# Down projection of a decoder step: low parts on VectorE, banks emptied by copies, late tiles, a five-step tail

## The chip, the cores and the metric

The kernel runs on one core of one Trainium2 chip. The metric is the device time of one execution in microseconds (us); of several executions the median is taken. An execution's time is a little longer than the span of its trace, which runs from the first to the last instruction.

## The reference

One decoder layer for 1024 prompt tokens and 64 sample tokens: token mixing, cross-attention and a gated convolutional FFN, each between RMSNorms. The change lies in the last matmul of the FFN and the norm and residual behind it:

```python
def conv_ffn(h, p, buf):
    ...
    gate, val = jnp.split(c, 2, axis=-1)
    y = (jax.nn.gelu(gate, approximate=True) * val) @ p['w_down']     # (1024 x 2816) @ (2816 x 1024)
    return y, ext[:, t:]
...
    y, buf_new = conv_ffn(rmsnorm(x, p['g_ffn_pre']), p, buf)
    x = x + rmsnorm(y, p['g_ffn_post'])
```

## The kernel before

The product for the prompt is done in the Strassen-Winograd way. The gated rows are a 2 x 2 matrix of blocks A11 to A22 (512 tokens by 1408), the weight is one of blocks B11 to B22 (1408 by 512), and seven block products P1 to P7 (in the code's order P1, P7, P6 and P4 by turns, P5, P2, P3) take the place of eight. Each block product has 11 steps over k, so that there are 77 steps. A step needs two factors of 128 x 512, which are sums or differences of blocks; `factors` (line 1829) makes them with `minus` (VectorE, line 1826) and splits each with `dsplit`: the high part is a rounding copy on ScalarE (line 1821), the low part is source minus high part (line 1822), on the engine that `factors` names. In each step the first factor's low part is on GpSimd (`G`), the second's on VectorE (`V`); P5 has a third split, for the samples, on GpSimd.

A step then gives 4 row tiles of 128 tokens, each three matmuls of 128x128 by 128x512 (`rows`, through `mm3`, lines 374 to 376: high x high, high x low, low x high). In P1, P5, P2 and P3 two matmuls for the sample tokens follow (`rows_s`, lines 1999 and 2000). So a step has 12 or 14 matmuls, and the stage has 12 x 77 + 2 x 44 = 1012.

Each tile adds up in one PSUM bank over its 11 steps. There are eight banks: four of kind `dtile`, three of kind `aux`, one `smp`. `BANKS` says which kind a product's tiles take. A product takes banks that an earlier product has left, so its first matmul in such a bank waits until `evac` or `evac_s` has emptied it. `evac` is a ScalarE copy for P1 and P7 (lines 2005 and 2007) and a VectorE add for the others (`plus`, line 1692); P6 has a GpSimd add behind it (line 2010). `evac_s` copies half of the sample bank on ScalarE (line 2023) and adds on VectorE.

Splits are made ahead: `run_factors` makes factors as long as the 11 pairs of buffers in `slots` suffice, which is five steps with the one in work (three in P5). Blocks come from memory by SyncE's queue: `hold` for those that stay, `stage` with five buffers for those that pass through (lines 1807 and 1814). The stage has no order by hand beyond the program's: a scheduler sets each engine's order, by its own model of time, and may place a subtraction well ahead of the step that needs it. Each engine's queue is worked off in order.

The last four steps of P3 are done tile by tile (`TAIL`), the samples first and then tiles 0 to 3. After a tile `last_rows` adds the bank to the row, takes the sum of squares on ScalarE (line 311), multiplies by the norm's gain on GpSimd (line 2056), and `post_norm` (lines 2037 to 2045) adds the residual on VectorE and writes out two halves.

Of the kernel before, what the change touches and what calls it, by code (L numbers as in the profile page):

```python
# [115 lines left out]
def tile_decoder_step(ctx, tc, cf, x_prompt, x_sample, cache_sb_k, cache_sb_v, state_hgrn,  # L116
# [6 lines left out]
    V, S, G, PE, SP = nc.vector, nc.scalar, nc.gpsimd, nc.tensor, nc.sync  # L123
# [100 lines left out]
    def f32(ap):  # L224
        return ap.bitcast(F32)
# [1457 lines left out]
    def product(a, n, e=ALL, j=0, bank=dtile):  # L1683

        p = bank()[:, :256 * (e.stop - e.start)].rearrange("p (e t) -> p e t", t=256)
        c = slice(128 * j, 128 * (j + 1))
        for k in range(4):
            mm3(p, a[0][:, k, c], a[1][:, k, c], form(n, 0, k, e), form(n, 1, k, e), k == 0, k == 3)
        return p

    def plus(out, a, b):
        V.tensor_tensor(out=out, in0=a, in1=b, op=ALU.add)  # L1692
# [60 lines left out]
    for e in (EARLY, LATE):  # L1753
# [16 lines left out]
        p = product(s1, "T1", e)  # L1770
# [13 lines left out]
    slots = []  # L1784
# [4 lines left out]
    def unit(n, k):  # L1789
        return staged[n, k] if (n, k) in staged else at(held[n][k], [512])  # L1790
# [12 lines left out]
    def hold(n, k):  # L1803

        m = min(2, 11 - k)
        place = "A11" if n == "A12" else n
        SP.dma_start(out=at(held[place][k], [m, 512]), in_=source(n, k, m))
# [10 lines left out]
    def dsplit(src, eng):  # L1818
        hi, lo = slots[slot[0] % len(slots)]
        slot[0] += 1  # L1820
        S.copy(out=hi, in_=src)
        eng.tensor_tensor(out=lo, in0=src, in1=f32(hi), op=ALU.subtract)  # L1822
        return hi, lo

    def minus(out, a, b, op=ALU.subtract):
        V.tensor_tensor(out=out, in0=a, in1=b, op=op)  # L1826
        return out

    def factors(name, k):

        if name == "P1":
            return dsplit(unit("A11", k), G), dsplit(unit("B11", k), V)
        if name == "P7":
            t = minus(dtmp(), unit("B22", k), unit("B12", k))
            return dsplit(unit("S3", k), G), dsplit(t, V)
        if name == "P6":
            t = minus(dtmp(), unit("B22", k), unit("B12", k))
            t = minus(unit("B11", k), t, unit("B11", k), ALU.add)
            return dsplit(unit("S2", k), G), dsplit(t, V)
        if name == "P4":  # L1840
            t = minus(unit("B21", k), unit("B21", k), unit("B11", k))
            return dsplit(unit("A22", k), G), dsplit(t, V)
        if name == "P5":
            a = minus(unit("A11", k), unit("A11", k), unit("S2", k), ALU.add)
            t = minus(unit("B11", k), unit("B12", k), unit("B11", k))
            return dsplit(a, G), dsplit(t, V), dsplit(unit("B12", k), G)
        if name == "P2":
            return dsplit(unit("A11", k), G), dsplit(unit("B21", k), V)
        a = minus(unit("A11", k), unit("A11", k), unit("S2", k))
        return dsplit(a, G), dsplit(unit("B22", k), V)  # L1850

    slot = [0]
    dtmp = Rot([at(Y0 + 8 * D + 512 * i, [512]) for i in range(2)])
    steps = [(n, k) for ns in (["P1"], ["P7"], ["P6", "P4"], ["P5"], ["P2"], ["P3"]) for k in range(11) for n in ns]
    STAGED = {"P1": ["B11"], "P7": ["S3"], "P6": ["B11", "A22", "B21"], "P5": ["B11"], "P2": ["B21"]}

    passing = []
# [5 lines left out]
    flight, ready = [], {}  # L1863
    nload, nprep = [0], [0]

    def run_loads():

        flight[:] = [x for x in flight if x >= nprep[0]]
        while nload[0] < len(passing) and len(flight) < len(stage_off):
            b, k, last = passing[nload[0]]  # L1870
            stage(b, k)
            if last < 11:
                hold("A11", k)
            flight.append(last)
            nload[0] += 1

    def run_factors(limit=99):

        while nprep[0] < min(len(steps), limit):
            n, k = steps[nprep[0]]  # L1880
            if sum(len(x) for x in ready.values()) + 2 + (n == "P5") > len(slots):
                break
            run_loads()
            ready[nprep[0]] = factors(n, k)
            nprep[0] += 1
            if n in ("P5", "P2") and k % 2 == 0:
                j = k - 4 if n == "P5" else k + 8
                if 0 <= j < 11:
                    hold("A12", j)
# [33 lines left out]
    for g in range(1, NGRP):  # L1923
# [23 lines left out]
        p = product(s1, "T1", bank=bank)  # L1947
# [39 lines left out]
    C1, C2_ = slice(0, 512), slice(512, 1024)  # L1987
    tiles, sacc = {}, {}

    def rows(name, j, k, f):  # L1990
        t = slice(128 * j, 128 * (j + 1))
        mm3(tiles[name][j], f[0][0][:, t], f[0][1][:, t], f[1][0], f[1][1], k == 0, k == 10)

    def rows_s(name, k, f):
        w = f[2] if name == "P5" else f[1]
        if k == 0:
            sacc[name] = smp()
        kk = k + 11 * (name in ("P2", "P3"))
        PE.matmul(sacc[name], gS[:, kk, :], w[0], start=k == 0, stop=False)  # L1999
        PE.matmul(sacc[name], gS[:, kk, :], w[1], start=False, stop=k == 10)  # L2000

    def evac(name, j):
        p, y1, y2 = tiles[name][j], Y[j], Y[4 + j]
        if name == "P1":
            S.copy(out=y1[:, C1], in_=p)
        elif name == "P7":
            S.copy(out=y2[:, C2_], in_=p)
        elif name == "P6":
            plus(y1[:, C2_], p, y1[:, C1])
            G.tensor_tensor(out=y2[:, C2_], in0=y2[:, C2_], in1=y1[:, C2_], op=ALU.add)  # L2010
        elif name == "P4":
            plus(y2[:, C1], p, y2[:, C2_])
        elif name == "P5":
            plus(y1[:, C2_], p, y1[:, C2_])
            plus(y2[:, C2_], p, y2[:, C2_])
        elif name == "P2":
            plus(y1[:, C1], p, y1[:, C1])
        else:
            plus(y1[:, C2_], p, y1[:, C2_])

    def evac_s(name):
        y, p, t = yS2[name in ("P5", "P3")], sacc[name], dtmp()[:64]
        S.copy(out=t, in_=p[64:128])
        if name in ("P1", "P5"):
            plus(y, p[0:64], t)
        else:
            plus(t, p[0:64], t)
            plus(y, y, t)
# [26 lines left out]
    def gain(y, cs, eng=V):  # L2055
        eng.tensor_tensor(out=y, in0=y, in1=gB[:y.shape[0], cs], op=ALU.mult)
# [28 lines left out]
    def last_rows(j):  # L2085
        if j == 4:
            evac_s("P3")
            square(yS2[1], stS[:64, 1:2])
            gain(yS2[1], C2_)
            yield  # L2090
            post_norm(64, yS2, [stS[:64, i:i + 1] for i in range(2)], xsrow[0], ys)
            return
        evac("P3", j)
        y = Y[j]
        square(y[:, C2_], st2[:, 4 + j:5 + j])
        gain(y[:, C2_], C2_, G)
        yield
        post_norm(128, [y[:, C1], y[:, C2_]], [st2[:, i:i + 1] for i in (j, 4 + j)], xrow[j], yp[j * 128:(j + 1) * 128, :])

# [2 lines left out]
    for j in range(6):  # L2102
        for b in ("B22", "B12"):
            ahead.setdefault(max(0, 3 + 2 * j), []).append((b, 2 * j))
        ahead.setdefault(13 + 4 * j, []).append(("S2", 2 * j))
    TAIL = len(steps) - 4
    side = iter(())
    for i, (n, k) in enumerate(steps[:TAIL]):
        run_factors()
        j = ahead.get(i, ())  # L2110
        for b in j:
            hold(*b)
        if k == 0:
            tiles[n] = [b() for b in BANKS[n]]
        for j in range(4):
            rows(n, j, k, ready[i])
        if n in ("P1", "P2", "P5", "P3"):
            rows_s(n, k, ready[i])
        del ready[i]
        if k == 10:  # L2120
            for j in range(4):
                evac(n, j)
            if n in ("P1", "P2", "P5"):
                evac_s(n)
            if n == "P5":
                load_bcast(gB, g_ffn_post)
                for j in range(4):
                    fetch(4 + j, xrow[j])
                side = second_rows()
            if n == "P2":  # L2130
                for _ in side:
                    pass
                fetch(8, xsrow[0])
                side = first_rows()
        if n == "P1" and k == 2:
            last_tokens()
        if n == "P1" and k == 4:
            sample_rows(11)
        next(side, None)
# [1 line left out]
        pass  # L2141
    run_factors()
    live = []
    for j in (4, 0, 1, 2, 3):
        for i in range(TAIL, len(steps)):
            k = steps[i][1]
            if j == 4:
                rows_s("P3", k, ready[i])
            else:
                rows("P3", j, k, ready[i])  # L2150
        step(live)
        live.insert(0, last_rows(j))
        step(live)
# [39 lines left out]
```

## Time and profile before

| | us |
|---|---|
| median of 3 runs | 1985.63 |
| lowest, highest | 1978.38, 1988.15 |
| the profiled execution | 1981.71 |
| its span in the trace | 1979.9 |
| span of the stage, from P1's first matmul | 1713.7 to 1979.9 |

In a timeline row the first number is the start, the second the duration of the group, and brackets hold how long the engine sat idle before it and what ended that. Matmul durations overlap: one shown with 0.39 us leaves the next to start some 0.23 us later. In a row of stretches the clock is a share of 2.4 GHz, so that 0.50 would be a whole stretch at 1.2 GHz.

### The profile page before, as it was taken

To read this page: it belongs to the slowest core of one execution; us is meant where nothing else is said; L and a number is where in the kernel's file an instruction comes from. 1 tells how busy PE (TensorE), PEld (TensorE's weight loads), DVE (VectorE), ACT (ScalarE), POOL (GpSimd) and SP (SyncE) were. 2 spreads that over 40 slices of the span, in tenths; PEclk is the share of its full clock that TensorE was granted. 3 is DMA by queue.
4 is the path that set the end of the run, shared out by engine and by line. 5 is a ranking of instruction groups with operands and counts; after the bars stand their busy time and mean duration, and the time that the engine had idled before them with its cause. 6 is when DMAs were issued, how large, how long until landed. Compare 5 with 4: busy or idle time off the path is not lost. (4 is left out here: it accounts for less than half of the span.)

```text
span 1979.9 us, 28696 instructions
## 1 busy us (share of the span) xinstructions
PE 1847.7 (93%) x10270; PEld 1493.8 (75%) x10270; DVE 1479.0 (75%) x2343; ACT 918.6 (46%) x1726; POOL 674.5 (34%) x552
## 2 busy tenths in 40 slices
PE   7998999998999899999899996899999999999897
PEld 6777877876887566777787775788888888887775
DVE  6587686678658675665655479889899899878695
ACT  6554364364346443344444345444444444544443
POOL 3102202202201322000400014655655655556884
PEclk9999899999899999999999998899999999999998
DMA  6211211111112655564226643222223333474531
GB/s 196 60 40 39 63 35 49 51 46 57 45 62 71 193 187 179 158 226 146 62 85 198 199 139 107 63 80 80 81 88 101 106 98 101 161 282 140 190 129 48
DMA packets 185388, 219.84 MB, mean 111 GB/s; under 512 B 24962, under 2 KB 116502, under 8 KB 184918
## 3 DMA queue, kind: packets, MB, share of 16 engines
q1 hardware_dynamic: 185246, 218.01, 34.9%
q8 instruction: 81, 1.33, 0.3%
q14 instruction: 61, 0.50, 0.1%
HBM read 171.19 MB, written 47.13 MB: 110 GB/s over the span
## 5 line engine op out<-in xcount | busy, mean ns | idle before, releaser
L374 PE MATMUL d<-act,arena_r 128*128 128x512 f32 (+1 forms) x640 | 257.4, 402 | 8.0 <-DVE arena_f L1692 6.3
L375 PE MATMUL d<-act,arena_r 128*128 128x512 f32 (+1 forms) x640 | 253.4, 396 | 0.0
L376 PE MATMUL d<-act,arena_r 128*128 128x512 f32 (+1 forms) x640 | 252.9, 396 | 0.3 <-DVE arena_r L1559 0.3
L374 PE MATMUL d<-arena_r,act 128*128 128x512 f32 (+1 forms) x576 | 205.1, 358 | 0.1
L375 PE MATMUL d<-arena_r,act 128*128 128x512 f32 (+1 forms) x576 | 202.4, 351 | 0.9 <-DVE arena_r L354 0.8
L376 PE MATMUL d<-arena_r,act 128*128 128x512 f32 (+1 forms) x576 | 202.7, 352 | 0.0
L1559 POOL TENSOR_TENSOR ffn_s<-arena_f,ffn_s 128x512 fp32r<-128x512 f32 x87 | 153.0, 1768 | 132.1 <-ACT ffn_s L1558 132.1
L1729 DVE SCALAR_TENSOR_TENSOR arena_f<-arena_f 128x64 f32<-128x64 f32 (+2 forms) x176 | 189.2, 1105 | 2.4 <-ACT arena_f L1727 1.4
L354 POOL TENSOR_TENSOR arena_r<-arena_f,arena_r 128x1024 fp32r<-128x1024 f32 (+1 forms) x34 | 81.3, 2398 | 266.5 <-ACT arena_r L353 230.4
L374 PEld LDWEIGHTS d<-act,arena_r 128*128 128x128 f32 x640 | 122.5, 191 | 33.1 <-DVE arena_f L1692 6.5
L353 ACT CAST arena_r<-arena_f 128x1024 fp32r<-128x1024 f32 (+1 forms) x96 | 98.6, 1028 | 98.9 <-PE d L376 21.7
L376 PEld LDWEIGHTS d<-act,arena_r 128*128 128x128 f32 x640 | 121.6, 190 | 26.9 <-DVE arena_r L1559 0.5
L375 PEld LDWEIGHTS d<-act,arena_r 128*128 128x128 f32 x640 | 122.0, 191 | 23.2
L1692 DVE TENSOR_TENSOR arena_f<-d,arena_f 128x512 f32<-128x512 f32 (+1 forms) x173 | 111.8, 661 | 25.6 <-PE d L376 21.6
L374 PEld LDWEIGHTS d<-arena_r,act 128*128 128x128 f32 x576 | 110.2, 192 | 20.7 <-issue 6.9
L354 DVE TENSOR_TENSOR arena_r<-arena_f,arena_r 128x1024 fp32r<-128x1024 f32 (+1 forms) x62 | 74.5, 1203 | 66.5 <-ACT arena_r L353 66.5
L375 PEld LDWEIGHTS d<-arena_r,act 128*128 128x128 f32 x576 | 110.1, 191 | 17.1 <-DVE arena_r L354 2.1
L376 PEld LDWEIGHTS d<-arena_r,act 128*128 128x128 f32 x576 | 110.1, 191 | 15.2 <-issue 2.5
L1559 POOL TENSOR_TENSOR arena_r<-arena_f,arena_r 128x1024 fp32r<-128x1024 f32 (+1 forms) x44 | 106.1, 2428 | 23.9 <-ACT arena_r L1558 23.8
L1727 ACT ACTIVATE arena_f<-arena_f 128x64 f32<-128x64 f32 (+1 forms) x88 | 69.4, 836 | 45.1 <-DVE arena_f L1692 44.9
L1559 POOL TENSOR_TENSOR ffn_T<-ffn_f,ffn_T 128x512 fp32r<-128x512 f32 x12 | 20.1, 1678 | 189.7 <-ACT ffn_T L1558 189.7
L1679 DVE TENSOR_TENSOR arena_f<-arena_f 128x512 f32<-128x512 f32 x84 | 78.3, 933 | 4.2 <-POOL ffn_s L1559 3.5
(580 smaller groups left out, 4964.4 us busy)
## 6 DMA issues: line engine op xcount, KB each, us to landing
arena_f<-in_w_up_dram SPq DMA_DIRECT2D x88, 256.0 KB, 3.1
arena_f<-in_w_in_dram SPq DMA_DIRECT2D x52, 256.0 KB, 3.4
gd<-arena_f SPq DMA_DIRECT2D x22, 512.0 KB, 2.6
arena_f<-in_w_o_dram SPq DMA_DIRECT2D x16, 512.0 KB, 4.1
arena_f<-in_w_cq_dram SPq DMA_DIRECT2D x16, 512.0 KB, 3.8
arena_f<-in_cache_mem_k_dram SPq DMA_DIRECT2D x32, 256.0 KB, 3.4
arena_f<-in_w_co_dram SPq DMA_DIRECT2D x16, 512.0 KB, 3.9
arena_f<-in_cache_mem_v_dram SPq DMA_DIRECT2D x32, 256.0 KB, 4.1
```

Of the source, the lines that this page charges most:

```text
L353: newest[0] = S.copy(out=hi, in_=raw)
L354: lo_engine().tensor_tensor(out=lo, in0=raw, in1=f32(hi), op=ALU.subtract)
L374: PE.matmul(p, ah, bh, start=first, stop=False)
L375: PE.matmul(p, ah, bl, start=False, stop=False)
L376: PE.matmul(p, al, bh, start=False, stop=last)
L1559: eng.tensor_tensor(out=dst[1], in0=src, in1=f32(dst[0]), op=ALU.subtract)
L1679: eng.tensor_tensor(out=o, in0=a, in1=b, op=op)
L1692: V.tensor_tensor(out=out, in0=a, in1=b, op=ALU.add)
L1727: S.activation(out=c, in_=taps[2], func=AF.Identity, scale=cw[:, 2, m:m + 1], bias=cw[:, 3, m:m + 1])
L1729: V.scalar_tensor_tensor(out=outs[i], in0=taps[i], scalar=cw[:, i, m:m + 1], in1=outs[i], op0=ALU.mult, op1=ALU.add)
```

## The change

- `factors`: the first factor's low part goes from GpSimd to VectorE in all 77 steps. P5's third split stays on GpSimd.
- The last steps of P6 and P4 are put in another order: P6's steps 9 and 10, then P4's 9 and 10. P6 ends two steps before P4, not one.
- `run_factors` counts buffers from the oldest step still needed, as steps are no longer released in order.
- P6's `evac` becomes a ScalarE copy out of the bank and a VectorE add from SBUF.
- `BEHIND`: in P5, P2 and P3, tile 3 and the samples of step 0 are done in step 1, behind the tiles 0 to 2 of step 1.
- P7's tile 3 is emptied first (`ORDER`), and `evac_s` follows directly behind tile 0's `evac`.
- The tail has five steps, not four, in the order tile 0, samples, tiles 1 to 3; its gain for the second half of a row is on VectorE.

```diff
         if name == "P1":
-            return dsplit(unit("A11", k), G), dsplit(unit("B11", k), V)
+            return dsplit(unit("A11", k), V), dsplit(unit("B11", k), V)
...
-            return dsplit(a, G), dsplit(t, V), dsplit(unit("B12", k), G)
+            return dsplit(a, V), dsplit(t, V), dsplit(unit("B12", k), G)
...
-    slot = [0]
+    slot, taken = [0], {-1: 0}
...
-    steps = [(n, k) for ns in (["P1"], ["P7"], ["P6", "P4"], ["P5"], ["P2"], ["P3"]) for k in range(11) for n in ns]
+    steps = [(n, k) for n in ("P1", "P7") for k in range(11)]
+    steps += [(n, k) for k in range(9) for n in ("P6", "P4")]
+    steps += [("P6", 9), ("P6", 10), ("P4", 9), ("P4", 10)]
+    steps += [(n, k) for n in ("P5", "P2", "P3") for k in range(11)]
...
-            if sum(len(x) for x in ready.values()) + 2 + (n == "P5") > len(slots):
+            if slot[0] - taken[min(ready, default=-1)] + 2 + (n == "P5") > len(slots):
                 break
             run_loads()
+            taken[nprep[0]] = slot[0]
             ready[nprep[0]] = factors(n, k)
+            taken[-1] = slot[0]
...
         elif name == "P6":
-            plus(y1[:, C2_], p, y1[:, C1])
+            S.copy(out=y1[:, C2_], in_=p)
+            plus(y1[:, C2_], y1[:, C2_], y1[:, C1])
             G.tensor_tensor(out=y2[:, C2_], in0=y2[:, C2_], in1=y1[:, C2_], op=ALU.add)
...
-        gain(y[:, C2_], C2_, G)
+        gain(y[:, C2_], C2_)
...
-    TAIL = len(steps) - 4
+    TAIL = len(steps) - 5
+    SAMPLED = ("P1", "P2", "P5", "P3")
+
+    BEHIND = {"P5": (3, 4), "P2": (3, 4), "P3": (3, 4)}
+    ORDER = {"P7": (3, 0, 1, 2)}
+
+    def job(i, j):
+        n, k = steps[i]
+        if j < 4:
+            rows(n, j, k, ready[i])
+        elif n in SAMPLED:
+            rows_s(n, k, ready[i])
...
-        for j in range(4):
-            rows(n, j, k, ready[i])
-        if n in ("P1", "P2", "P5", "P3"):
-            rows_s(n, k, ready[i])
-        del ready[i]
+        late_ = BEHIND.get(n, ()) if k == 0 else ()
+        done_ = [j for j in range(5) if j not in late_]
+        if lag and n == lag[0][0]:
+
+            i0, js = lag.pop()[1:]
+            for j in done_:
+                if j not in js:
+                    job(i, j)
+            for j in js:
+                job(i0, j)
+                job(i, j)
+            del ready[i0]
+        else:
+            for j in done_:
+                job(i, j)
+        if late_:
+            lag.append((n, i, late_))
+        else:
+            del ready[i]
         if k == 10:
-            for j in range(4):
+            for j in ORDER.get(n, range(4)):
                 evac(n, j)
-            if n in ("P1", "P2", "P5"):
-                evac_s(n)
+                if j == 0 and n in ("P1", "P2", "P5"):
+                    evac_s(n)
...
-    for j in (4, 0, 1, 2, 3):
+    for j in (0, 4, 1, 2, 3):
         for i in range(TAIL, len(steps)):
-            k = steps[i][1]
-            if j == 4:
-                rows_s("P3", k, ready[i])
-            else:
-                rows("P3", j, k, ready[i])
+            job(i, j)
```

## Rows read from the trace of the kernel before

**Rows 1.** The page's first line.
```profile
span 1979.9 us, 28696 instructions
```

**Rows 2.** Stretches: length, then busy us and instructions by engine, clock, DMA share, GB/s.
```profile
1780.60:1851.20 70.60, 63.16 (x265) 50.47 (x263) 63.90 (x73) 28.80 (x53) 43.21 (x24) 0.96 0.51 159
1851.20:1888.90 37.70, 37.65 (x154) 30.44 (x155) 22.19 (x22) 17.71 (x33) 36.70 (x25) 0.94 0.58 197
...
1968.60:1979.90 11.30, 0.00 (x0) 0.00 (x0) 8.19 (x18) 2.44 (x8) 2.66 (x2) 0.63 0.44 162
```

**Rows 3.** Stretches behind three of the matmul waits: PE, PEld, VectorE, ScalarE, GpSimd, clock.
```profile
1785.80:1790.50 4.70, 4.65 (x14) 3.66 (x15) 4.70 (x9) 2.13 (x5) 3.59 (x1) 0.64 0.88 280
...
1851.20:1855.50 4.30, 4.25 (x10) 3.38 (x11) 4.30 (x7) 0.00 (x0) 4.30 (x4) 0.51 0.03 13
...
1933.70:1937.50 3.80, 3.75 (x10) 2.97 (x10) 3.44 (x7) 2.69 (x8) 3.80 (x3) 0.55 0.00 0
```

**Rows 4.** Timeline of TensorE: all its waits from 1713 us on, and two pitch marks.
```profile
1785.85 0.50 PE L374 MATMUL d<-arena_r,ffn_s 128*128 128x512 f32 x1 [2.30 <-ACT arena_f L2007]
...
1851.25 0.77 PE L374 MATMUL d<-arena_r 128*128 128x512 f32 x1 [5.18 <-DVE arena_f L1692]
...
1893.28 0.50 PE L374 MATMUL d<-arena_r 128*128 128x512 f32 x1 [2.14 <-DVE arena_f L1692]
...
1897.47 0.50 PE L1999 MATMUL smp<-arena_r,ffn_T 128*128 128x512 f32 x1 [1.58 <-DVE arena_f L1692]
...
1933.75 0.66 PE L1999 MATMUL smp<-arena_r,ffn_T 128*128 128x512 f32 x1 [1.99 <-DVE st L2053]
...
1939.14 0.40 PE L374 MATMUL d<-arena_r 128*128 128x512 f32 x1
...
1968.20 0.39 PE L376 MATMUL aux<-ffn_s,arena_r 128*128 128x512 f32 x1
```

**Rows 5.** Timeline of VectorE and GpSimd where they run side by side, or alone.
```profile
1797.88 1.73 POOL L1822 TENSOR_TENSOR arena_r<-dn_w,arena_r 128x512 fp32r<-128x512 f32 x1
1798.39 3.48 DVE L1826 TENSOR_TENSOR arena_f<-arena_f,dn 128x512 f32<-128x512 f32 x2
...
1814.62 1.28 DVE L1826 TENSOR_TENSOR dn<-arena_f,dn 128x512 f32<-128x512 f32 x2
...
1851.18 5.49 POOL L2010 TENSOR_TENSOR arena_f<-arena_f 128x512 f32<-128x512 f32 x4 [7.00 <-DVE arena_f L1692]
...
1852.22 0.68 DVE L1692 TENSOR_TENSOR arena_f<-smp,arena_f 128x512 f32<-128x512 f32 x1
1852.81 1.44 DVE L1822 TENSOR_TENSOR ffn_T<-arena_f,ffn_T 128x512 fp32r<-128x512 f32 x1
```

**Rows 6.** Timeline of ScalarE at the end of P7.
```profile
1783.20 0.62 ACT L1821 CAST arena_r<-dn 128x512 fp32r<-128x512 f32 x1 [1.76 <-DVE dn L1826]
...
1785.20 0.60 ACT L2007 COPY arena_f<-d 128x512 f32<-128x512 f32 x1
```

**Rows 7.** Timeline of VectorE at the end of P4.
```profile
1849.21 0.69 DVE L1826 TENSOR_TENSOR arena_f<-dn_w,arena_f 128x512 f32<-128x512 f32 x1 [0.86 <-DMA arena_f<-in_w_down_dram]
```

**Rows 8.** Timeline of VectorE at the end of P5.
```profile
1892.55 4.26 DVE L1692 TENSOR_TENSOR arena_f<-d,arena_f 128x512 f32<-128x512 f32 x7
1896.74 0.67 DVE L1692 TENSOR_TENSOR arena_f<-smp,arena_f 64x512 f32<-64x512 f32 x1
```

**Rows 9.** Timeline of VectorE and GpSimd in the tail, last tile.
```profile
1971.66 0.68 DVE L1692 TENSOR_TENSOR arena_f<-aux,arena_f 128x512 f32<-128x512 f32 x1
...
1972.64 2.42 DVE L2044 SCALAR_TENSOR_TENSOR dn_w<-arena_f,rs_y,dn_w 128x512 f32<-128x512 f32 x2
1973.17 1.33 POOL L2056 TENSOR_TENSOR arena_f<-arena_f,dn_w 128x512 f32<-128x512 f32 x1 [2.12 <-ACT dn_w L311]
...
1975.62 1.41 DVE L2044 SCALAR_TENSOR_TENSOR dn_w<-arena_f,rs_y,dn_w 128x512 f32<-128x512 f32 x2
```

More of the change, by code (lines that the diff above doesn't have):

```diff
@@ L1831, in factors @@
         if name == "P1":
-            return dsplit(unit("A11", k), G), dsplit(unit("B11", k), V)
+            return dsplit(unit("A11", k), V), dsplit(unit("B11", k), V)
         if name == "P7":
             t = minus(dtmp(), unit("B22", k), unit("B12", k))
-            return dsplit(unit("S3", k), G), dsplit(t, V)
+            return dsplit(unit("S3", k), V), dsplit(t, V)
         if name == "P6":
@@ L1838, in factors @@
             t = minus(unit("B11", k), t, unit("B11", k), ALU.add)
-            return dsplit(unit("S2", k), G), dsplit(t, V)
+            return dsplit(unit("S2", k), V), dsplit(t, V)
         if name == "P4":
             t = minus(unit("B21", k), unit("B21", k), unit("B11", k))
-            return dsplit(unit("A22", k), G), dsplit(t, V)
+            return dsplit(unit("A22", k), V), dsplit(t, V)
         if name == "P5":
@@ L1845, in factors @@
             t = minus(unit("B11", k), unit("B12", k), unit("B11", k))
-            return dsplit(a, G), dsplit(t, V), dsplit(unit("B12", k), G)
+            return dsplit(a, V), dsplit(t, V), dsplit(unit("B12", k), G)
         if name == "P2":
-            return dsplit(unit("A11", k), G), dsplit(unit("B21", k), V)
+            return dsplit(unit("A11", k), V), dsplit(unit("B21", k), V)
         a = minus(unit("A11", k), unit("A11", k), unit("S2", k))
-        return dsplit(a, G), dsplit(unit("B22", k), V)
-    slot = [0]
+        return dsplit(a, V), dsplit(unit("B22", k), V)
+    slot, taken = [0], {-1: 0}
     dtmp = Rot([at(Y0 + 8 * D + 512 * i, [512]) for i in range(2)])
-    steps = [(n, k) for ns in (["P1"], ["P7"], ["P6", "P4"], ["P5"], ["P2"], ["P3"]) for k in range(11) for n in ns]
+    steps = [(n, k) for n in ("P1", "P7") for k in range(11)]
+    steps += [(n, k) for k in range(9) for n in ("P6", "P4")]
+    steps += [("P6", 9), ("P6", 10), ("P4", 9), ("P4", 10)]
+    steps += [(n, k) for n in ("P5", "P2", "P3") for k in range(11)]
     STAGED = {"P1": ["B11"], "P7": ["S3"], "P6": ["B11", "A22", "B21"], "P5": ["B11"], "P2": ["B21"]}
@@ L2105, in tile_decoder_step @@
         ahead.setdefault(13 + 4 * j, []).append(("S2", 2 * j))
-    TAIL = len(steps) - 4
+    TAIL = len(steps) - 5
[8 more added lines that the diff above has]
+            rows_s(n, k, ready[i])
     side = iter(())
+    lag = []
     for i, (n, k) in enumerate(steps[:TAIL]):
```

## The prediction

> **What bounds the kernel now.** I read first where TensorE waits in this stage, then the clock behind each wait, then what the engine named by the wait was doing, and last the stretch behind the last matmul. TensorE has five waits of note, and all stand where a product takes over banks: 2.30 us at P4's first step (for P7's copy), 5.18 at P5's, 2.14 and 1.58 in P2's and 1.99 in P3's first step; together 13.2 us [rows 4]. Elsewhere matmuls follow each other at (1968.20 - 1939.14) / 125 = 0.2325 us, 125 being the matmuls that start from the one row to the other [rows 4], so the 1012 matmuls need 235 us and the stage is near that bound but for the handovers.
>
> Three waits cost more than their own length. Behind them the granted clock of the stretch is 0.64, 0.51 and 0.55 [rows 3], the last two near the lower level of 1.2 GHz: 14 matmuls in 4.70 us that need 3.25, 10 in 4.30 and 10 in 3.80 that need 2.33. That is 1.45 + 1.97 + 1.47 = 4.9 us. An idle time is counted from a modelled end 0.39 us after a start, where the next start is due after 0.23, so each wait has 0.16 more. By place: P4's start 3.9, P5's 7.3, P2's 4.0, P3's 3.6; 18.9 us in all.
>
> Who is late? VectorE. At P7's end the copy that frees the bank stands on ScalarE behind a rounding copy that waited 1.76 us for a VectorE subtraction [rows 6]. At P4's end VectorE waits for a weight transfer [rows 7] with the adds that free P6's banks queued behind it. At P5's end seven adds run in a row from 1892.55, with the sample bank's add only behind them at 1896.74 [rows 8]. And VectorE is slow because GpSimd works beside it: two subtractions that take 1.28 us alone (0.60 to the next, 0.68 by itself) take 3.48 while GpSimd is at its low parts [rows 5]. During P6 and P4 VectorE is busy 63.9 of 70.6 us, during P5 GpSimd 36.7 of 37.7 [rows 2].
>
> The last matmul starts at 1968.20; from its end the span runs on for 11.3 us without any [rows 2, 4].
>
> **The change part by part.** Low parts. 77 leave GpSimd for VectorE. GpSimd spends 1.73 us on one where both are busy, VectorE 0.60 when alone [rows 5], and each of VectorE's neighbours loses up to 1.74 - 0.60 = 1.1 us to it. In P6 and P4, VectorE has 73 instructions now and gets 22: 95 x 0.60 = 57 us, where TensorE needs 22 steps x 12 x 0.2325 = 61.4. In P5 it goes from 22 to 33, which is 20 us of 36 (154 matmuls), with 11 low parts of 1.73 still on GpSimd. So this gives no time of its own, since TensorE waits for no factor within a product; it pays for the rest. Its bounds: nothing at 0.60 us, and what the second rival gives if the mean stays high.
>
> P7's order and copy: tile 3's bank is wanted 12 matmuls (2.8 us) after P7's end and is now copied first, in 0.60 us [rows 6]. Even if ScalarE is held up by 1.76 us as now, that makes 2.4 us. P4's wait goes: -3.9.
>
> P5's start. P6 ends 24 matmuls (5.6 us) before P5, and its banks are emptied by four ScalarE copies of 0.60, so the three banks for P5's tiles 0 to 2 and the samples' are free in time, unless ScalarE is itself stuck behind VectorE. Tile 3's bank is P4's, emptied by a VectorE add, but is wanted only after two times three tiles (18 matmuls, 4.2 us). VectorE can still be late with it, by a transfer: P4's steps 9 and 10 now follow directly, so the weight block of step 10 is asked for one step later than before. The waits for transfers that I see are up to about a microsecond [rows 7], and the factors lead by four steps, some 11 us. I allow 0 to 5 us, and take 2.5. P5: -7.3 + 2.5. If P6's copies on ScalarE lose their cover, each costs 0.60.
>
> Against that, P6's second add now reads two SBUF operands. Such an add stretched to 1.44 beside GpSimd's four adds of P6, while the add out of a bank just before took 0.68 [rows 5]. At worst the four cost 4 x 1.1 = 4.6 us on VectorE, covered by the 5.6 us. The Trainium skill, "SBUF — State Buffer", section "SBUF: two separate sides", says that a VectorE instruction with two SBUF inputs and a GpSimd instruction take one shared port pair by an exclusive lock, held for the whole instruction. It speaks against this edit, and the rows agree: the bank add beside GpSimd at 0.68, the SBUF ones at 1.44 and 1.74. By it the four adds would cost their full 4.6 us, which the two steps still cover; the sum stays the same.
>
> P2's and P3's start. In P2 the bank for tile 3 comes from P5's tile 0, and `evac_s` now stands directly behind that tile's adds. Tile 3 is wanted 18 matmuls (4.2 us) after P5's end, the samples 24 (5.6 us). The first add now starts at 1892.55 [rows 8]. P5 ended some 4.4 us before TensorE's wait ended at 1893.28 (nine matmuls, 2.1 us, and the 2.3 of the wait), at 1888.9. Even with VectorE as late as now, tile 3's bank is free near 1893.2, 0.1 us late, and the sample bank near 1894.5 where it is wanted. In P3 the sample bank was had at 1933.75, 2.79 + 2.1 us after P2's end, and is wanted 5.6 after. Both go: -4.0 and -3.6. The matmuls that are put off are the same in number, so the reordering costs nothing on TensorE.
>
> Tail. TensorE's pace per tile goes from 12 to 15 matmuls, 2.79 to 3.49 us. VectorE's per tile is now the pair of residual adds, 2.42 beside GpSimd's gain against 1.41 alone [rows 9], 0.60 for the bank and some 0.6 for small ones (1975.06 to 1975.62): 3.6, more than TensorE's 2.79, so it falls behind. The last bank add starts at 1971.66, 3.1 us after the last matmul's end at 1968.59. After: 1.41 + 0.60 + 0.60 (the gain) + 0.6 = 3.2, less than 3.49, so VectorE keeps up. From the last bank add to the end of the last pair it is now 1975.62 + 1.41 - 1971.66 = 5.4 us, of which the tile before, at 2.42 for 1.41, gives 1.0 back: 4.4, and 2.9 for the output. The add starts 0.1 to 0.95 us after the last matmul, the latter behind the earlier tile's pair. Sum 7.3 to 8.2 against 11.3: -3.1 to -4.0, I take -3.6. A step more in the tail wants its last factors later: the last split can begin as the step before the tail ends and needs two copies and a low part, about 2 us, where tile 0 wants it after four steps, 2.8 us. No cost, but little room.
>
> P1's low parts move into the end of the up projection, where VectorE has other work; no TensorE wait falls there now, and I cost it at nothing.
>
> **Sum.** Against the profiled execution's 1981.7, which is 1.8 more than its span of 1979.9 [rows 1]: - 18.9 + 2.5 - 3.6 = 1961.7, so 1962. That execution is 3.9 under the median of the runs shown, between the lowest and the median; I don't shift the sum, and let the range take that in.
>
> **Rivals.** (1) VectorE becomes the bound inside products. If its mean comes out at 0.75 us, P6 and P4 need 95 x 0.75 = 71 us for 61.4: 10 us of new waits, and 1972. For it: 57 of 61.4 leaves little air, and P5's remaining GpSimd low parts stretch four VectorE operations a step. Against: no such wait now, with more time lost to GpSimd, and many of these subtractions are made ahead and could be made later.
>
> (2) Slower: VectorE keeps nearly its present mean, because what stretches it isn't GpSimd. In P6 and P4 it is 63.9 / 73 = 0.875 us [rows 2]. Then 95 of them need 83 us, 22 over; P7 and P5 fit; the handovers stay late (no 18.9 back), and only the tail gives: 1981.7 + 22 - 3.6 = 2000. It decides above 61.4 / 95 = 0.65 us, and the result passes to slower from (61.4 + 18.9 + 3.6) / 95 = 0.88 on if the handovers go, at once if they don't. Against: 0.60 where GpSimd rests.
>
> (3) The change doesn't do what it says: copies and adds that free banks stay behind VectorE's late work, since ScalarE's queue is held by its subtractions [rows 6]. Then P4's and P5's waits stay, 11.2 us, without my allowance of 2.5: 1961.7 + 8.7 = 1970; with P2's as well, 1974.
>
> **How the numbers follow.** Forecast 0.62, (1) 0.18, (2) 0.06, (3) 0.14. The forecast's own range is 1954 (nothing of the 2.5, the tail's 4.0, runs like the lowest shown) to 1968 (5 us at P5's start and the median's 3.9). The range goes to 1977 to take in (1) and (3). A measurement of this kernel can tell about 0.5% from no change, so faster is under 1975.7: all of the forecast, two thirds of (1) and half of (3): 0.81. Within 0.5%: the rest of those, 0.13. Slower: (2), 0.06.
>
> **What would show it.** Right: no TensorE wait over 1 us at the five places and no stretch near 0.5 of the clock; VectorE's subtractions in P6 and P4 near 0.60 to 0.70 us; GpSimd's busy time in the stage down by more than half; about 7 to 8 us behind the last matmul. Wrong: TensorE waits for a low part on VectorE inside a product (1, 2), a copy of P6 on ScalarE that starts after P4's end (3), or a wait at P5's start over 5 us with a transfer at its root.

## The result and the profile after

The changed kernel takes 1962.87 us in the median of 4 runs (1957.22 to 1965.01), the kernel before 1985.63 in the same comparison: a ratio of 0.9884 with a 95% interval of 0.9859 to 0.991. The forecast was 1962. The sum of the prediction came out, in part by luck; the parts of the change that were to earn it did not.

The page of the kernel after, its first line and the busy time of the engines:

```profile
span 1955.4 us, 28621 instructions
...
PE 1838.5 (94%) x10270; PEld 1486.2 (76%) x10270; DVE 1474.8 (75%) x2424; ACT 923.7 (47%) x1730; POOL 538.5 (28%) x471
```

The span is 24.5 us shorter than [rows 1]. It divides in three: 2.2 lie ahead of the stage, where only P1's first low parts were moved (P1's first matmul starts at 1713.73 before, 1711.52 after, and anywhere from 1711.52 to 1723.33 in the runs below, so I take this for scatter); the stage, here from P1's first matmul to the end of the last, goes from 254.86 to 235.97, so 18.9; and the tail, which is what follows it, goes from 11.31 to 7.91, so 3.4.

One row of the stretches covers the stage: length, then busy us and instructions of PE, PEld, VectorE, ScalarE and GpSimd, clock, DMA share, GB/s. First before, then after:

```profile
1713.70:1968.60 254.90, 241.66 (x1014) 193.13 (x1012) 200.06 (x252) 113.74 (x224) 167.45 (x96) 0.97 0.47 157
```
```profile
1711.50:1947.50 236.00, 235.52 (x1014) 189.68 (x1012) 196.75 (x334) 117.34 (x230) 38.21 (x21) 1.00 0.50 171
```

These two lines are the case. VectorE does 82 instructions more and is busy 3.3 us less: 0.794 us an instruction before, 0.589 after. GpSimd is busy 129 us less, and VectorE paid nothing for it. In P6 and P4 alone, where the prediction put 95 instructions at 57 us, it has 94 in 57.2 (the stretch after):

```profile
1778.10:1839.30 61.20, 61.20 (x266) 49.63 (x265) 57.23 (x94) 28.49 (x52) 9.79 (x1) 1.00 0.51 168
```

A group that both kernels have, VectorE's sums and differences of weight blocks, shows it in one operation (count, busy us, mean ns, idle time before); before, then after:

```profile
L1826 DVE TENSOR_TENSOR dn<-dn,dn_w 128x512 f32<-128x512 f32 x16 | 17.0, 1089 | 1.2 <-POOL arena_r L1822 1.2
```
```profile
L1826 DVE TENSOR_TENSOR dn<-dn,dn_w 128x512 f32<-128x512 f32 x16 | 10.3, 685 | 0.0
```

TensorE's waits in the stage, by what ended them (us in total, times, longest), are one line where [rows 4] had five places:

```profile
PE d L375 <- DVE ffn_s L1822: 0.5, 1, 0.5
```

It doesn't lie at a handover but inside P5, in its fifth step: P5's first matmul starts at 1839.26, the wait ends at 1853.23. The granted clock of the whole stage is 1.00, so no stretch like [rows 3] is left. The gaps between matmul starts that are longer than the pitch of 0.2325 us exceed it by 1.5 us in all, where it was 20.5.

ScalarE at P7's end (the rows that answer to [rows 6]; a line is start, duration, engine, line, operation, tile, and in brackets the idle time before and what ended it):

```profile
1776.23 0.59 ACT L2014 COPY arena_f<-aux 128x512 f32<-128x512 f32 x1
...
1777.23 1.08 ACT L2014 COPY arena_f<-aux 128x512 f32<-128x512 f32 x2
...
1778.71 0.61 ACT L2014 COPY arena_f<-d 128x512 f32<-128x512 f32 x1
```

`ORDER` puts tile 3, the one in a `d` bank, first in the program; on the engine its copy is still the last of four, 0.4 us after P7's last matmul ends (1778.29). TensorE's wait for it is gone all the same: before, ScalarE stood 1.76 us for a VectorE subtraction at this place [rows 6], and here it doesn't.

GpSimd and VectorE at P4's end (answering to [rows 7] and to the GpSimd adds of [rows 5]):

```profile
1829.51 9.90 POOL L1822 TENSOR_TENSOR ffn_s<-dn_w,ffn_s 128x512 fp32r<-128x512 f32 x1 [113.93 <-DMA dn<-in_w_down_dram]
...
1841.86 1.29 POOL L1822 TENSOR_TENSOR arena_r<-dn_w,arena_r 128x512 fp32r<-128x512 f32 x1
```
```profile
1833.35 1.90 DVE L1692 TENSOR_TENSOR arena_f<-arena_f 128x512 f32<-128x512 f32 x3
...
1840.69 0.69 DVE L1692 TENSOR_TENSOR arena_f<-d,arena_f 128x512 f32<-128x512 f32 x1 [2.44 <-POOL arena_f L2018]
```

What was left on GpSimd is now the slow part: one low part stretches over 9.90 us while VectorE works without a gap, against 1.29 at 1841.86, and the adds of P6 stand behind it. VectorE waits 2.44 us for one of them before it can empty P4's bank. P5's start, for which the prediction allowed 2.5 us for a late transfer, lost nothing. Some 0.8 us were lost 10 to 14 us later inside P5, to the low part on VectorE shown above, which came late behind these waits.

### The profile page after: what moved, and what is told of

Same layout as the page of the kernel before. It is cut to its first block, busy times and chain, and to the rows that moved or that the text cites. A ratio compares the mean times of both kernels' runs of the same rounds, so it can differ in the third digit from the quotient of the medians.

```text
span 1955.4 us, 28621 instructions
## 1 busy us (share of the span) xinstructions
PE 1838.5 (94%) x10270; PEld 1486.2 (76%) x10270; DVE 1474.8 (75%) x2424; ACT 923.7 (47%) x1730; POOL 538.5 (28%) x471
## 5 line engine op out<-in xcount | busy, mean ns | idle before, releaser
L660 ACT ACTIVATE mix_f<-aux,arena_f 128x384 f32<-128x384 f32 (+3 forms) x96 | 56.4, 587 | 39.6 <-PE aux L658 18.2
```

The lines of the kernel that those rows point to most:

```text
L660: a1 = table("sig", S.activation(out=un[:, :w], in_=z[:, :w], func=AF.Sigmoid, bias=nbiasB[:, h:h + 1], scale=-SB_SC))
```

## The experiments

All runs but the first two are the kernel after with a part undone, moved or added, or the kernel before with parts of the change. Each ratio is to the kernel before as run beside it. Stage and tail as defined above; "lost" is the sum of what the gaps between the stage's matmul starts exceed the pitch of 0.2325 by, to some 0.3 us (shorter gaps are not set against it). The time is the median; stage, tail and "lost" come from one profiled execution of each run, and that isn't always near the median: those of after (1957.22) and e6 (1962.10) are the shortest of their four.

| run | time, ratio to before (95%) | stage | tail | lost in the stage, by place |
|---|---|---|---|---|
| before | 1985.63 | 254.86 | 11.31 | 20.5: P4 4.4, P5 7.3, P2 4.3, P3 3.8 |
| after | 1962.87, 0.9884 (0.9859 to 0.991) | 235.97 | 7.91 | 1.5 |
| e1 low parts back on GpSimd | 1984.05, 0.9997 (0.9982 to 1.0011) | 255.85 | 7.76 | 21.3: 4.4, 8.1, 6.1, 1.9 |
| e2 low parts alone | 1965.89, 0.9899 (0.9854 to 0.9944) | 235.58 | 11.38 | 1.2 |
| e3 no late tiles | 1961.15, 0.9872 (0.9844 to 0.99) | 236.71 | 7.96 | 2.3 |
| e4 tail as before | 1966.85, 0.9903 (0.9871 to 0.9934) | 236.68 | 11.46 | 2.3 |
| e7 low parts and tail alone | 1963.62, 0.9894 (0.9857 to 0.993) | 236.19 | 7.97 | 1.8 |
| e8 low parts of P6 and P4 alone | 1975.97, 0.9958 (0.9936 to 0.9981) | 243.74 | 11.67 | 9.4: 0, 1.9, 4.5, 2.2 |
| e5 idle adds, holding buffers | 2028.04, 1.0224 (1.0177 to 1.027) | 300.08 | 7.91 | 66.1 |
| e6 idle fills | 1968.89, 0.9941 (0.9905 to 0.9977) | 238.26 | 7.93 | 4.4 |
| e10 idle adds, tied loosely | 1974.46, 0.9955 (0.9935 to 0.9974) | 245.71 | 8.16 | 15.7 |
| e9 nothing on GpSimd | 1961.64, 0.9882 (0.9855 to 0.991) | 235.32 | 7.78 | 1.0 |
| e11 tail's gain on GpSimd | 1960.86, 0.9878 (0.9839 to 0.9916) | 236.02 | 11.23 | 1.6 |
| e12 tail's gain moved, order as before | 1962.12, 0.9875 (0.9806 to 0.9945) | 237.11 | 9.42 | 2.7 |

**e1: everything but the low parts.** The kernel after, with `factors` as before.

```diff
-            return dsplit(unit("A11", k), V), dsplit(unit("B11", k), V)
+            return dsplit(unit("A11", k), G), dsplit(unit("B11", k), V)
...
```

> The changed kernel with the first factor's low parts back on GpSimd; all the rest of the change stays. My theory: VectorE is slow again beside GpSimd, yet the late tiles and the early copies give 4 to 6 us of air at each handover, so most of the 18.9 us of handover loss stays away: P2's and P3's waits gone, 2 to 7 us left at P4's and P5's start. From P1's first matmul to the last one's end some 240 us (254.9 before, 236.0 changed), time about 1968. Rival, that the low parts pay for everything: the handover waits return nearly whole, 250 us or more, time about 1979.

The stage is no shorter than before (255.85 against 254.86): late tiles, copies of P6, the new orders and the early `evac_s` gain nothing by themselves, and the rival of the expectation came. P4's, P5's and P2's waits are there again, the last two at their new places:

```profile
1787.14 0.50 PE L374 MATMUL d<-arena_r,ffn_s 128*128 128x512 f32 x1 [2.32 <-ACT arena_f L2014]
...
1856.72 0.79 PE L374 MATMUL d<-arena_r 128*128 128x512 f32 x1 [3.35 <-DVE arena_f L1692]
...
1898.72 0.79 PE L374 MATMUL d<-arena_r 128*128 128x512 f32 x1 [3.27 <-DVE arena_f L1692]
```

The reason is to be read on VectorE at P5's end, where P5's last matmul ends at 1891.3:

```profile
1888.77 0.69 DVE L1826 TENSOR_TENSOR dn<-dn,dn_w 128x512 f32<-128x512 f32 x1 [4.94 <-POOL arena_r L1822]
...
1889.44 1.72 DVE L2064 TENSOR_TENSOR arena_f<-arena_f,dn_w 128x512 f32<-128x512 f32 x1
1891.09 1.78 DVE L1822 TENSOR_TENSOR arena_r<-arena_f,arena_r 128x512 fp32r<-128x512 f32 x1
1892.80 3.47 DVE L1826 TENSOR_TENSOR dn<-dn,dn_w 128x512 f32<-128x512 f32 x2
...
1897.99 2.47 DVE L1692 TENSOR_TENSOR arena_f<-d,arena_f 128x512 f32<-128x512 f32 x4
```

VectorE first waits 4.94 us for a GpSimd low part (1.19 before), then does a run of operations at 1.7 us each, and comes to the row of adds that free the banks 6.7 us after P5's end. Before, it was 3.65 ([rows 8]: 1892.55 against 1888.9). The bank is wanted 2.1 us later (18 matmuls after P5's end, not nine), and the adds come 3.05 us later.

**e2: the low parts alone.** The kernel before, with only `factors` as after.

```diff
-            return dsplit(unit("A11", k), G), dsplit(unit("B11", k), V)
+            return dsplit(unit("A11", k), V), dsplit(unit("B11", k), V)
...
```

> The kernel before with the 77 low parts on VectorE and nothing else of the change. My theory: VectorE's two-operand work in P6 and P4 falls from a mean near 0.9 to 0.6 to 0.7 us, it is no longer late, and the waits at P4's, P2's and P3's start shrink to under 1 us each; P5's stays at 1 to 4 us, since P6's banks are emptied by VectorE adds only one step ahead. P1's first matmul to the last one's end 238 to 243 us, tail 11 us as before, time about 1972. Rival, that moving low parts alone overloads VectorE or does nothing: 254 us or more, time 1983 to 2000.

All five waits close to 0.4 us or less, with the tiles in their old places and P6 emptied by adds, P5's too, where I had expected 1 to 4 us. The stage is 235.58. P5's last matmul ends at 1879.5, and the adds have begun before it:

```profile
1878.23 4.86 DVE L1692 TENSOR_TENSOR arena_f<-d,arena_f 128x512 f32<-128x512 f32 x8
```

In the kernel after they begin at 1874.72 with P5's end at 1876.0, so in both 1.3 us ahead of it. e1 and e2 together show that the stage's gain is that of the low parts.

**e3 and e4: late tiles and tail undone.** `BEHIND = {}` in the one; the old tail (four steps, samples first, gain on GpSimd) in the other.

> The changed kernel with no tiles put off (tile 3 and the samples of step 0 back in step 0 in P5, P2 and P3). From the changed trace: P5's tile 3 would be wanted 2.1 us after P4's end and its bank is free 1.4 us after it; the sample banks are free 1 to 2 us before they would be wanted. My theory now: no wait over 1 us at any of the three, stage 236 to 238 us, time as the changed kernel's (ratio to before 0.988 to 0.990). The prediction's own account, in which putting off gives P2 and P3 back 7.6 us: 240 us or more and a time about 5 to 8 us above the changed kernel's.

> The changed kernel with the old tail: four steps tile by tile, samples first, gain on GpSimd. My theory: the stretch behind the last matmul goes from 7.9 us back to 11.3 and nothing else moves: time 3.4 us above the changed kernel's. Rival, that the tail is shorter because VectorE comes to it with no work left over: 8 to 9 us behind the last matmul.

Without late tiles the time is 1961.15, which can't be told from after. The old tail costs 3.55 us of tail and nothing else that can be told from scatter.

**e7: low parts and tail alone.** The kernel before with those two parts, and without late tiles, P6's copies and both new orders.

> The kernel before with two parts of the change: the 77 low parts on VectorE and the new tail (five steps, tile 0 before the samples, gain on VectorE). No late tiles, no P6 copies, no new order of P6 and P4, old order of emptying. My theory after the first four runs: this is the whole gain: stage 235.5 to 237 us, 7.8 to 8.0 us behind the last matmul, the changed kernel's time within 3 us (1958 to 1966 by the median). Rival, that late tiles and copies matter once the tail is new: 3 us or more above it.

1963.62 against 1962.87, stage 236.19, tail 7.97: the whole gain, as far as it can be measured, with two of the seven parts.

**e8: low parts of P6 and P4 alone.** The kernel before with `V` for the first factor in these two products.

> The kernel before with only P6's and P4's 22 low parts on VectorE. My theory: each handover is late by the VectorE work of the product before it. P5's wait (7.3 us) goes to under 1.5; P4's (4.4), at the end of P7, and P3's (3.8), at the end of P2, stay within 1 us of that; P2's (4.2) may shrink by up to half. Stage 245 to 249 us. Rival, that GpSimd's lateness is carried over from product to product: less than half of P5's wait goes, 250 us or more.

The stage is 243.74, shorter than the 245 to 249 expected: it gives 11.1 of 18.9, of which 9.8 at P4's and P5's start. Of P5's wait a rest is left, and P2's and P3's stay as waits; the low parts of P5 and P2, the products ahead of them, are still on GpSimd:

```profile
1853.73 0.50 PE L374 MATMUL d<-arena_r 128*128 128x512 f32 x1 [1.37 <-DVE arena_f L1692]
...
1892.06 0.50 PE L374 MATMUL d<-arena_r 128*128 128x512 f32 x1 [2.38 <-DVE arena_f L1692]
```

P4's wait stands behind P7, whose low parts were not moved, and I had not counted on its going. The factors of P6 and P4 are made some steps ahead, so theirs may be the work that lies around P7's end; no run shows it apart. P3's wait is as long as before (1.98 us against 1.99), yet its place loses 1.6 us less, as the granted clock behind it stays at 1.00, where it was 0.55 in [rows 3]:

```profile
1932.50:1936.30 3.80, 3.77 (x16) 3.08 (x17) 3.44 (x7) 3.03 (x9) 3.80 (x3) 1.00 0.00 0
```

**e5, e6, e10: idle work on GpSimd.** Is VectorE slowed by what GpSimd does, or was TensorE waiting for GpSimd's late results? To part the two, idle GpSimd work, of which no result uses anything, is put beside each step's first factor in the kernel after. e5: a copy of one column of the factor, and two subtractions of 128x256 from SBUF.

```diff
+        if ghost:
+            G.tensor_copy(out=gtick[:, 0:1], in_=f32(hi)[:, 0:1])
+            [G.tensor_tensor(out=gout, in0=gid, in1=gid, op=ALU.subtract) for _ in range(2)]
```

> The changed kernel, with idle work added on GpSimd behind each of the 77 moved low parts: a read of one column of the factor's high part, then two subtractions of a constant from itself (128x256 each, two SBUF operands) into a scratch that nobody reads. VectorE's instructions are those of the changed kernel. My theory, that a GpSimd instruction beside them is what made VectorE late: the mean of VectorE's 128x512 subtractions in the P6 and P4 stretch goes from 0.6 to 0.7 us back to 0.85 or more, TensorE waits return, P1's first matmul to the last one's end 245 to 275 us against 236.0. Rival, that the gain came from GpSimd's slow low parts no longer being waited for: nothing waits for the idle work, so 236 to 239 us.

e6: the same with two memsets of the same bytes in place of the subtractions.

> As the run with idle subtractions, but GpSimd fills the scratch twice (memset, 128x512 bf16) and reads nothing for it but the one column. If what stretches VectorE is GpSimd reading SBUF beside it, VectorE's mean stays at 0.6 to 0.7 us and the stage within 236 to 239 us. If any GpSimd instruction does it, the stage comes out between the changed kernel's and the run with idle subtractions, 242 us or more. The Trainium skill, SBUF - State Buffer, section SBUF: two separate sides, says that a VectorE instruction with two SBUF inputs shuts out, and is shut out by, only a GpSimd instruction that reads SBUF; by that nothing changes here.

e5 lost 64 us of stage, but not to what it was made for. GpSimd runs its idle work in long rows, and the column it copies belongs to a factor's buffer, which ScalarE can't overwrite until then (GpSimd's timeline, then a line of the waits: us in total, times, longest):

```profile
1779.66 24.46 POOL L1829 TENSOR_TENSOR ffn_T<-arena_f 128x256 fp32r<-128x256 f32 x35
```
```profile
ACT arena_r L1825 <- POOL gtick L1828: 53.5, 11, 23.9
```

So its time settles nothing. In e6 GpSimd is as busy as before the change (163.86 us of the stage against 167.45), yet VectorE does a subtraction in 683 ns and the stage is 238.26 (groups: count, busy us, mean ns, idle time before):

```profile
L1829 POOL MEMSET ffn_T<- 128x512 bf16 x144 | 75.4, 524 | 6.7
...
L1833 DVE TENSOR_TENSOR arena_f<-dn_w 128x512 f32<-128x512 f32 x22 | 14.5, 683 | 0.0
```

Over the whole stage VectorE's 336 instructions take 199.5 us, against 334 in 196.8. In this execution a busy GpSimd that reads next to nothing (one column a step) hardly slows VectorE. The median, 1968.89, is 6 us above after's all the same, and why the other three executions took 1968.75 to 1979.27 isn't shown, as they have no trace. That leaves a GpSimd that reads. e10 puts the mark in a column of its own, written by ScalarE, so that no factor's buffer is held, and runs one 128x256 subtraction with that column:

```diff
+        if idle:
+            S.copy(out=m, in_=f32(hi)[:, 0:1])
...
+            G.tensor_tensor(out=gout, in0=gid, in1=m[:, None, :].to_broadcast([128, 2, 128]), op=ALU.subtract)
```

> The kernel after, with idle work added that no result of the kernel uses: beside each step's first factor ScalarE also copies one column into a column of its own, and GpSimd runs one 128x256 subtraction of two SBUF operands that needs that column and holds no factor's buffer. GpSimd has then about as much to do in a step as in the kernel before, but nobody waits for it; the idle work that the first such run held back through a shared buffer is taken out of the case. Theory A (VectorE lost its time because GpSimd read SBUF beside it): VectorE's subtractions of factors rise from 0.68 to a mean of 0.9 to 1.2 us, the waits of TensorE behind the handovers come back, and the stage is 245 us or more against 235.97; time 1972 or more. Theory B (the waits came from waiting for GpSimd's late results, of which there are none here): the means may rise, but the stage stays at 236 to 239 us and the time at 1963 to 1967.

Its stage as a row of stretches, to be held against after's:

```profile
1723.30:1969.00 245.70, 233.66 (x1014) 190.26 (x1012) 227.91 (x332) 127.33 (x305) 129.16 (x94) 0.98 0.48 164
```

VectorE's 332 instructions take 227.9 us in place of 196.8: 91 us more of busy GpSimd, whose idle results nobody waits for, take 31 us from VectorE. (26 of the 91 are a single idle subtraction that was held up. The means of VectorE's larger groups are 0.73 to 0.89; the 0.9 to 1.2 expected was too much.) The stage is 9.7 us longer, and lost more than that: undisturbed matmuls follow each other at a mean of 0.227 us in this run, 0.232 in after, which gives back some 5 us; no run shows why. Most of the loss is one wait of 9.08 at P5's start, for the add that frees tile 3's bank. VectorE has no wait for GpSimd in this stage, and comes to that add by 21 instructions without a gap, in 20.0 us where 0.60 each would be 12.6. So stretching is enough to bring a late handover back. It isn't a clean price: just ahead of the 21, VectorE had waited 2.53 us for a weight transfer.

**e9: nothing left on GpSimd.** P5's third low part, P6's second add and the first rows' gain on VectorE too.

```diff
-            return dsplit(a, V), dsplit(t, V), dsplit(unit("B12", k), G)
+            return dsplit(a, V), dsplit(t, V), dsplit(unit("B12", k), V)
...
-            G.tensor_tensor(out=y2[:, C2_], in0=y2[:, C2_], in1=y1[:, C2_], op=ALU.add)
+            plus(y2[:, C2_], y2[:, C2_], y1[:, C2_])
...
-            gain(Y[j][:, C1], C1, G)
+            gain(Y[j][:, C1], C1)
```

> The kernel after with what was left on GpSimd in the steps put on VectorE as well: P5's third low part, the additions of P6's tiles, the gain on the first rows. Theory A (work on GpSimd beside VectorE costs VectorE about what it takes off it): VectorE's time in the last stage grows by less than 10 us, the stage is 235 to 236.5 us, the wait at P5's start (a low part of 9.9 us on GpSimd) is gone, and the time is within 2 us of the kernel after. Theory C (VectorE is near its bound in P5, where five operations of a step then lie on it at 0.68 us against a step of 3.1 us): waits of 1 to 5 us in all come up inside P5, stage 237 to 241.

```profile
1717.80:1953.10 235.30, 235.20 (x1014) 189.74 (x1012) 198.13 (x355) 117.91 (x233) 1.50 (x2) 1.00 0.51 172
```

21 more instructions cost VectorE 1.4 us, TensorE has no wait in the stage, and 1011 pitches of 0.2325 are 235.1 of its 235.3 us. The time, 1961.64, can't be told from after's 1962.87. It is the simplest of the versions at this time.

**e11, e12: the tail in halves.** e11 puts the last rows' gain back on GpSimd and keeps the new order; e12 keeps the gain on VectorE and takes the old order back.

```diff
-        gain(y[:, C2_], C2_)
+        gain(y[:, C2_], C2_, G)
```
```diff
-    TAIL = len(steps) - 5
+    TAIL = len(steps) - 4
...
-    for j in (0, 4, 1, 2, 3):
+    for j in (4, 0, 1, 2, 3):
```

> The kernel after with one operation put back: the gain on the short tile's second half at the end is on GpSimd again. The prediction's step was that of the 3.6 us of the tail 1.0 comes from VectorE's pair of tile 2 running undisturbed (1.41 in place of 2.42 us) and the rest from the order of the last tiles. If so the tail is 8.5 to 9.2 us against 7.91. If the order alone did it, or the pair then lies ahead of that operation, it stays at 7.8 to 8.2. The stage is unchanged at 236.

> The kernel after with the order of the last tiles as before (the short tile ahead of the others at the end, four steps laid out tile by tile) and only the gain on VectorE kept. With the gain back on GpSimd and the new order the tail was 11.23 us, against 7.91 after and 11.31 before: the order alone gave nothing. If the operation on GpSimd is all of it (it stretches the pair beside it and the last bank's addition stands behind that pair in VectorE's order), the tail here is 7.7 to 8.5 us and the span that of the kernel after within its scatter. If both are needed (the last tiles too close together in the old order), it is 9.5 to 11.5. The stage is 235.5 to 237 in either case.

The tail is 11.31 us before, 11.23 with the order alone (8.5 to 9.2 was expected), 9.42 with the gain alone (just under the 9.5 to 11.5 expected if both were needed), 7.91 with both. Two executions each are too few to see 2 or 3 us in the time; the profiled tails show it, as tails of one make differ by 0.4 us at most among the runs (11.31 to 11.67 for the old one, 7.76 to 8.16 for the new). After, with the last matmul's end at 1947.49 (answering to [rows 9]):

```profile
1947.61 0.68 DVE L1692 TENSOR_TENSOR arena_f<-aux,arena_f 128x512 f32<-128x512 f32 x1
...
1948.46 1.41 DVE L2052 SCALAR_TENSOR_TENSOR dn_w<-arena_f,rs_y,dn_w 128x512 f32<-128x512 f32 x2
...
1951.11 1.41 DVE L2052 SCALAR_TENSOR_TENSOR dn_w<-arena_f,rs_y,dn_w 128x512 f32<-128x512 f32 x2
```

e11, with the last matmul's end at 1951.27:

```profile
1951.27 1.80 POOL L2064 TENSOR_TENSOR arena_f<-arena_f,dn_w 128x512 f32<-128x512 f32 x1 [3.34 <-ACT dn_w L311]
...
1953.58 1.42 DVE L2052 SCALAR_TENSOR_TENSOR dn_w<-arena_f,rs_y,dn_w 128x512 f32<-128x512 f32 x2
1954.91 0.69 DVE L1692 TENSOR_TENSOR arena_f<-aux,arena_f 128x512 f32<-128x512 f32 x1
```

In e11 the pairs of residual adds are at 1.42, undisturbed, and the tail is long all the same: in VectorE's queue the last bank's add stands behind tile 2's pair, which comes behind GpSimd's gain. It starts 3.64 us after the last matmul's end, where it starts 3.06 after it before, 1.35 in e12 and 0.12 after. From that add to the end it is 7.6 to 8.2 us in all four.

## Why the total was right and the reasons were not

**The low parts: the step that failed.** The prediction put them down as giving "no time of their own" and paying "for the rest". Its rate was right: it expected subtractions of 0.60 to 0.70 us, and the group above has 0.685. Its 57 us for P6 and P4 came at 57.2. It had even named the cause of VectorE's lateness, GpSimd beside it [rows 5]. But it used that only to show that the added work would fit, and didn't ask what a VectorE that is 0.2 us an instruction quicker does for the adds that free the banks. That is the whole 18.9: e2 has it without the rest (235.58 us of stage), e1 has the rest without it (255.85).

**Handovers: right in amount, credited to the wrong parts.** -3.9, -7.3, -4.0 and -3.6 were to come from P7's order, P6's copies, late tiles and the early `evac_s`. The stage gave 18.9 as summed, but e3 and e7 show those parts worth nothing measurable beside fast low parts, and e1 nothing without them. The working for P2 took VectorE "as late as now", as a fixed time. In e1 that lateness grew by 3.05 us, from 3.65 to 6.7, and the bank's later turn gave 2.1. A late engine's lateness is no constant by which a deadline can be put off. (The prediction read 1892.55 as P5's first add. One stands alone ahead of the row, at 1891.35 before; a tile takes two, so its 1893.2 for the free bank holds.) And `ORDER` didn't reach the engine: the copy came last, as in e7, which has no `ORDER`.

**P5's start: the 2.5 us allowed were not used.** Nothing was lost there; the 0.8 lost inside P5 go back to GpSimd's slow low part, not to a transfer. P6's second adds, costed at up to 1.1 us more each (4.6 in all, where 4 x 1.1 is 4.4), weren't stretched at all: three take 1.90 us together. It was GpSimd that was held up at that time.

**Tail: -3.6 forecast, -3.4 measured, split wrongly.** That VectorE's pace per tile was the matter was right. But 1.0 of it was put on the pair's 2.42 us becoming 1.41, and e11 has pairs of 1.42 and a tail no shorter. What counts is when the last add gets its turn, and neither half alone brings that about: 0.1 and 1.9 us singly, 3.4 together.

**Sum.** The profiled execution came at 1957.2 against a sum of 1961.7: 2.5 of the difference is the allowance, 2.2 the scatter ahead of the stage, and the tail takes 0.2 back. That the median, 1962.87, also lies beside the 1962 is in part luck: the forecast took 20.0 off an execution 3.9 under the median of before, and the median fell by 22.8. The prediction's signs of being right came, too: no wait over 1 us, no slow stretch, subtractions near 0.60 to 0.70 us, GpSimd's busy time down by more than half, 7.9 us behind the last matmul. They name what goes away and not what makes it go, so they couldn't tell its account from the right one.

**Rivals.** VectorE as the bound at 0.75 us did not come, but for its sign: one wait for a low part inside a product, the 0.5 in P5, where the prediction had seen GpSimd's remaining low parts stretch VectorE, against the 10 us of that rival. e9, with none left on GpSimd, has no such wait. VectorE keeping 0.875 in P6 and P4 did not come either; e10, with idle reading on GpSimd, goes some way to it, at a mean of 0.686 over the stage (0.794 before, 0.589 after) and 11.6 us over after. Banks that stay late, the third rival, is what e1 shows, but with the low parts on GpSimd.

**Open.** How the 18.9 divides between stretched operations and VectorE's direct waits for GpSimd (4.94 us in e1's rows) is not settled: e10 shows the first to be enough for 31 us of VectorE's time and some 10 of the stage, with a wait of 2.5 for a transfer in it. Each edit also lets the scheduler set new orders on the engines, and no run holds them as they were, so what a new order alone does is not parted from either.

## What to carry to other kernels

Work given to GpSimd to relieve VectorE can cost VectorE more than it saves, where both read SBUF: compare VectorE's busy time and instruction count over the whole stage, not the price of the instruction moved. When a term of a sum is "this pays for the rest", also ask what it does alone to the waits that the rest is meant to close. An order written in the program is worth what the engine's queue shows of it.

## What the runs showed of the hardware

**VectorE and GpSimd take whole turns.** In e10 VectorE's operations of 128x512 with two inputs have three lengths, by what GpSimd does beside it (timeline of both engines):

```profile
1860.63 1.70 POOL L2029 TENSOR_TENSOR arena_f<-arena_f 128x512 f32<-128x512 f32 x1
...
1861.14 1.75 DVE L1831 TENSOR_TENSOR arena_r<-dn,arena_r 128x512 fp32r<-128x512 f32 x1
...
1862.30 1.06 POOL L1833 TENSOR_TENSOR ffn_T<-arena_f,gmark 128x256 fp32r<-128x256 f32 x1
...
1862.81 1.09 DVE L1837 TENSOR_TENSOR dn<-dn_w,dn 128x512 f32<-128x512 f32 x1
...
1864.99 1.71 POOL L1831 TENSOR_TENSOR ffn_s<-dn_w,ffn_s 128x512 fp32r<-128x512 f32 x1
...
1865.50 0.68 DVE L1692 TENSOR_TENSOR arena_f<-d,arena_f 128x512 f32<-128x512 f32 x1
```

1.75 us beside a 128x512 operation, 1.09 beside a 128x256 one, and 0.68 beside a 128x512 one where VectorE itself reads a bank. The Trainium skill, "SBUF — State Buffer", section "SBUF: two separate sides", has a VectorE instruction with two SBUF inputs and a GpSimd one that reads SBUF exclude each other for a whole instruction; these rows agree, and so does e6, where GpSimd's fills only write.

**The turns aren't always fair.** GpSimd's low part, 1.29 us alone, took 9.90 at 1829.51 in after, while VectorE did 14 instructions without a gap from 1829.74 on; it ended 1.2 us after VectorE stopped. In e10 an idle subtraction, 0.61 us alone, took 26.19 at 1907.56 beside a VectorE that never stopped. Yet later in after, with both at work without a gap, neither is shut out (timeline of both):

```profile
1846.88 5.15 POOL L1822 TENSOR_TENSOR arena_r<-dn_w,arena_r 128x512 fp32r<-128x512 f32 x3
...
1847.38 1.78 DVE L1822 TENSOR_TENSOR ffn_s<-arena_f,ffn_s 128x512 fp32r<-128x512 f32 x1
1849.09 1.78 DVE L1826 TENSOR_TENSOR arena_f<-dn_w,arena_f 128x512 f32<-128x512 f32 x1
```

What decides between the two is not shown. A busy time of GpSimd can hold much waiting.
